# Splitting each query and key pair once on 128 partitions and stacking it by DMA inside SBUF, in a two-layer attention and ffn kernel

## The chip, the cores and the metric

One core of one Trainium2 chip. The metric is device time in microseconds (us) of one execution of the whole kernel, taken as the median of several runs; less is better.

## The reference, cut to what matters

A sequence of 512 tokens of width 1024 (batch 1) goes through two layers; each is an attention block and a gated ffn (width 2816, a causal convolution of three taps on the gate), each behind an rmsnorm and with a residual. Heads are 64 wide. Layer 0 has 8 FOX heads (causal attention with a learned decay added to the scores) and 8 DSA heads (keys and values from a shared latent of rank 128; a small indexer of 4 heads picks the keys that each query may see). Layer 1 has 16 MoBA heads, which at this length come to causal attention. For each head:

```python
s = jnp.einsum('bqhd,bkhd->bhqk', q_i, k) * scale          # FOX: + c_i - c_k
s = jnp.where(mask, s, -jnp.inf)                           # causal, or the picked keys
p = jax.nn.softmax(s, axis=-1)
out = jnp.einsum('bhqk,bkhd->bqhd', p, v)
```

All is float32, the result 512 x 1024.

## The kernel before, in words

Activations lie transposed: features on 128 partitions, 512 tokens along the columns. A float32 operand is kept as two TensorE operands, a high part (a cast to fp32r on ACT) and a low part (the operand minus its high part, on DVE or POOL); `split` (L125) makes both. A projection (`proj`, L160) is 8 tiles of the input by three products (high·high, high·low, low·high; L154 to L156), so 24 matmuls of 128x512. Its weights come by `chunk` (L131): a DMA on SP's queue (`raw_...`, L142, 512 KB, three buffers), a cast on ACT (L143), a subtraction on DVE (L149), or in layer 0's heads on POOL (L147).

Two heads make a pair: one projection gives q of both, head 0 on partitions 0 to 63 (`LO`), head 1 on 64 to 127 (`HI`); another gives k. A score product has only 64 rows to sum over, so the kernel fills all 128 partitions with it: q high above q low in one tile, k high twice in another, k low twice in a third, and two matmuls (L256, L257) give the sum of the four products. Tiles per pair: `stack_q` (L236) makes one for each head, `a` and `b`; `stack_k` (L245) makes `ah`, `al` for head 0 and `bh`, `bl` for head 1. q's parts are written where they belong, since ACT and DVE may write to other partitions than they read; k's are made on one half and copied to the other half by a DMA inside SBUF (L251), four for a pair. The indexer's `ik` (L510 to L514) is cast and subtracted twice, once for each half.

`soft` (L320) works a head's four blocks of 128 queries: scores into PSUM (two buffers), a masked copy with the row's maximum on DVE (L335, the `mx` rows), exp with the row's sum on ACT (L336), a reciprocal of the sum on DVE (L337), and the normalisation on POOL (L338). `mix` (L342) transposes the probabilities on PE (L358), splits them (L126, L127) and multiplies by the values (L367, L368).

`heads` (L444) sets the order in the program: the scores of a head, then some work for the next pair (`vals`, `ks`, `qs`: its value, key and query projections with their stacking), then `mix` of the head before. In layer 0 `select` puts rounds of DVE MAX8 and MATCH_REPLACE8 (L547, L548) among it. From this program order a scheduler makes an order for each engine and each queue, which the engines then follow strictly. In layer 1 there are eight pairs, `m0` to `m7`; their q is `mq`, their k `mk`, their values `mv` (`fq`, `fk`, `fv` of FOX; `dq`, `dk`, `dv` of DSA). The score of block 0 of pair 2, head 0 is `s_m20_0`.

Of the kernel before, what the change touches and what calls it, by code (L numbers as in the profile page):

```python
# [18 lines left out]
F32 = mybir.dt.float32  # L19
F32R = mybir.dt.float32r  # L20
I32 = mybir.dt.int32
AF = mybir.ActivationFunctionType
OP = mybir.AluOpType
# [4 lines left out]
NB = T // P  # L28
# [43 lines left out]
def hybrid_kernel(ctx: ExitStack, tc: tile.TileContext, xT_d, pos_d, const_d, vec_d, w_d, out_d, idx):  # L72
    nc = tc.nc
    V, A, G, PE = nc.vector, nc.scalar, nc.gpsimd, nc.tensor
# [7 lines left out]
    def big(name):  # L82
        return ap_.tile([P, T], F32R, tag="big", name=name, bufs=N_BIG)
# [7 lines left out]
    def col(name, n=1):  # L91
        return tp.tile([P, n], F32, tag=f"col{n}", name=name, bufs=N_COL)
# [32 lines left out]
    def split(dst_h, dst_l, src, eng=V):  # L125
        A.copy(dst_h, src)  # L126
        eng.tensor_tensor(dst_l, src, dst_h.bitcast(F32), op=OP.subtract)  # L127
# [101 lines left out]
    def halves(y, nm, eng=V):  # L229
        h, l = big(f"{nm}_h"), big(f"{nm}_l")  # L230
        split(h, l, y, eng)
        return h, l

    LO, HI = slice(0, 64), slice(64, 128)

    def stack_q(y, nm):  # L236

        a, b = big(f"{nm}_a"), big(f"{nm}_b")
        A.copy(a[LO], y[LO])
        A.copy(b[HI], y[HI])  # L240
        V.tensor_tensor(a[HI], y[LO], a[LO].bitcast(F32), op=OP.subtract)
        V.tensor_tensor(b[LO], y[HI], b[HI].bitcast(F32), op=OP.subtract)
        return a, b

    def stack_k(y, nm, eng=V):  # L245

        ks = [big(f"{nm}_{n}") for n in ("ah", "bh", "al", "bl")]
        for e, (r, q) in enumerate(((LO, HI), (HI, LO))):
            split(ks[e][r], ks[2 + e][r], y[r], eng)
            for t in (ks[e], ks[2 + e]):  # L250
                nc.sync.dma_start(t[q].bitcast(F32), t[r].bitcast(F32))  # L251
        return ks

    def scores(out, q, k, e, qs, w, first=True):

# [64 lines left out]
    def soft(nm, e, q, k, bias, decay=None):  # L320

        probs = []
        prt = tp.tile([P, P * NB * (NB + 1) // 2], F32, tag="prt", name=f"prt_{nm}", bufs=N_PR)
        for i in range(NB):
            w = P * (i + 1)
            wm = max(w, 256)
            s = ps("S", f"s_{nm}_{i}")
            qs = slice(i * P, i * P + P)
            if decay is not None:
                sel, ck = decay  # L330
                PE.matmul(s[:, :wm], sel.to_broadcast([P, P]), ck[:, :wm], start=True, stop=False)
            scores(s[:, :wm], q, k, e, qs, wm, decay is None)
            neg = prt[:, P * i * (i + 1) // 2:P * (i + 1) * (i + 2) // 2]
            mx, sm = col(f"mx_{nm}_{i}"), col(f"sm_{nm}_{i}")
            V.tensor_tensor_reduce(neg, s[:, :w], bias[i], scale=-0.125, scalar=3e38, op0=OP.add, op1=OP.min, accum_out=mx)  # L335
            A.activation(neg, neg, AF.Exp, scale=-1.0, bias=mx, accum_out=sm)  # L336
            V.reciprocal(sm, sm)  # L337
            G.tensor_scalar(neg, neg, sm, 1.0, op0=OP.mult, op1=OP.mult)  # L338
            probs.append(neg)
        return probs  # L340

    def mix(nm, e, probs, v, hv, y):  # L342
# [165 lines left out]

    ym = rope(pmisc, "misc")
    ikh, ikl = big("ik_h"), big("ik_l")  # L510
    A.copy(ikh[0:64], ym[0:64])
    A.copy(ikh[64:128], ym[0:64])
    V.tensor_tensor(ikl[0:64], ym[0:64], ikh[0:64].bitcast(F32), op=OP.subtract)
    V.tensor_tensor(ikl[64:128], ym[0:64], ikh[0:64].bitcast(F32), op=OP.subtract)  # L514
    kr = big("kr")
    G.memset(kr[0:64].bitcast(F32), 0.0)
    split(kr[64:96], kr[96:128], ym[64:96])
# [1 line left out]
    t = ps("T", "iwps")  # L519
# [32 lines left out]
    y = scaled(proj("ckv"), "ckv")  # L552
    sq = tmp("sqkv")
    A.activation(sq, y, AF.Square)
    _, bc = rstd_of(sq, P, "kv")
# [258 lines left out]
```

## Time and profile before

| | |
|---|---|
| median of 3 runs | 1278.89 us (1277.62 to 1280.02) |
| profiled execution, its own time | 1276.6 us |
| span of its instructions | 1274.8 us |
| mean granted clock of TensorE | 0.994 |
| PE busy | 1224.2 us (96%), 6148 matmuls |
| DVE busy | 845.7 us (66%) |
| ACT busy | 591.7 us (46%) |
| POOL busy | 311.0 us (24%) |

How to read it: the metric is the device time of an execution, the span runs from the first to the last instruction of the profiled execution. Busy times are of the engine's own instructions; a share of the whole span is an average over stages. The stages lie about so: setup and first norm to 52 us, the eight pairs of layer 0 to 262, its output projection and norm to 292, the ffn to 648, norm and first projections of layer 1 to 675, its eight pairs to 880, output projection and norm to 910, ffn to 1262, and the last norm and output.

### The profile page before, as it was taken

How to read it: one execution, taken by the hardware profiler on the slowest of the kernel's cores; microseconds unless marked ns; L12 is line 12 of the kernel's file. 1: busy time of each engine (PE TensorE's matmuls, PEld its weight loads, DVE VectorE, ACT ScalarE, POOL GpSimd, SP SyncE). 2: the span in 40 equal slices, each digit the busy share in tenths (PEclk: the TensorE clock that was granted, in tenths of full speed). 3: DMA queues.
4: the chain of work that ended last, by engine and by line, in shares of the span. 5: the costliest groups of instructions: out<-in, count | busy, mean ns of one | idle time of the engine just before them, and what ended most of it. 6: DMA issues, size and time to landing. Idle time of an engine off the chain costs nothing.

```text
span 1274.8 us, 17004 instructions
## 1 busy us (share of the span) xinstructions
PE 1224.2 (96%) x6148; PEld 1024.0 (80%) x6148; DVE 845.7 (66%) x1629; ACT 591.7 (46%) x1011; POOL 311.0 (24%) x354
## 2 busy tenths in 40 slices
PE   6899989999999999999999999999999999999996
PEld 4778767778888888888888788778788888888896
DVE  7899998776555345554467879787755533665564
ACT  5585667654333123333336556556433321333443
POOL 3586656541110001110114323222111100111000
PEclk9999999999999999999999999999999999999998
DMA  5223222222333233333323232222233333223363
GB/s 191 67 77 106 76 59 73 61 73 93 99 99 99 92 91 99 99 100 99 100 90 93 85 97 68 82 83 67 83 100 99 99 99 98 88 97 99 118 189 107
DMA packets 37379, 120.95 MB, mean 95 GB/s; under 512 B 4736, under 2 KB 4864, under 8 KB 37296
## 3 DMA queue, kind: packets, MB, share of 16 engines
q1 hardware_dynamic: 36368, 118.51, 30.4%
q10 hardware_dynamic: 864, 1.17, 0.3%
q8 instruction: 48, 0.79, 0.3%
q14 instruction: 35, 0.29, 0.1%
q0 software_dynamic: 64, 0.20, 0.0%
HBM read 109.37 MB, written 2.10 MB: 87 GB/s over the span
## 4 chain that ended last, share of the span: by engine, by line
PE 79%; DVE 14%; ACT 3%; issue 3%; POOL 0%; DMA 0%; DVEq 0%; ACTq 0%; POOLq 0%
PE mm_d L155 6%; PE mm_d L154 6%; PE mm_d L156 6%; PE mm_u L156 6%; PE mm_u L155 6%; PE mm_u L154 6%; PE mm_g L155 6%; PE mm_g L154 6%; PE mm_g L156 6%; DVE tmask L548 1%; DVE xl L170 1%; PE o_m L367 1%; DVE m L547 1%; PE t_m L358 1%; PE o_m L368 1%
## 5 line engine op out<-in xcount | busy, mean ns | idle before, releaser
L422 POOL TENSOR_TENSOR cv<-cv,sg 128x512 f32<-128x512 f32 x44 | 56.9, 1293 | 543.0 <-ACT sg L421 543.0
L155 PE MATMUL mm_d<-a_l,wh_d 128*128 128x512 f32 (+1 forms) x440 | 152.7, 347 | 0.0
L156 PE MATMUL mm_d<-a_h,wl_d 128*128 128x512 f32 (+1 forms) x440 | 152.5, 347 | 0.0
L154 PE MATMUL mm_d<-a_h,wh_d 128*128 128x512 f32 (+1 forms) x440 | 152.5, 347 | 0.0
L155 PE MATMUL mm_g<-xl,wh_g 128*128 128x512 f32 x352 | 137.1, 390 | 0.0
L156 PE MATMUL mm_u<-xh,wl_u 128*128 128x512 f32 x352 | 137.1, 390 | 0.0
L154 PE MATMUL mm_g<-xh,wh_g 128*128 128x512 f32 x352 | 136.9, 389 | 0.0
L154 PE MATMUL mm_u<-xh,wh_u 128*128 128x512 f32 x352 | 136.9, 389 | 0.0
L155 PE MATMUL mm_u<-xl,wh_u 128*128 128x512 f32 x352 | 136.9, 389 | 0.0
L156 PE MATMUL mm_g<-xh,wl_g 128*128 128x512 f32 x352 | 136.9, 389 | 0.0
L143 ACT CAST wh_d<-raw_d 128x1024 fp32r<-128x1024 f32 x55 | 57.8, 1050 | 122.4 <-PE mm_d L155 83.5
L149 DVE TENSOR_TENSOR wl_d<-raw_d,wh_d 128x1024 fp32r<-128x1024 f32 x55 | 67.6, 1229 | 66.7 <-ACT wh_d L143 66.5
L143 ACT CAST wh_u<-raw_u 128x1024 fp32r<-128x1024 f32 x44 | 46.4, 1054 | 131.6 <-PE mm_g L155 114.6
L154 PEld LDWEIGHTS mm_d<-a_h,wh_d 128*128 128x128 f32 x440 | 83.3, 189 | 10.4
L156 PEld LDWEIGHTS mm_d<-a_h,wl_d 128*128 128x128 f32 x440 | 83.3, 189 | 10.3
L155 PEld LDWEIGHTS mm_d<-a_l,wh_d 128*128 128x128 f32 x440 | 83.3, 189 | 10.2
L417 DVE TENSOR_TENSOR gs<-mm_g,RB 128x512 f32<-128x512 f32 x44 | 30.4, 692 | 90.7 <-PE mm_g L156 90.2
L424 DVE TENSOR_TENSOR us<-mm_u,RB 128x512 f32<-128x512 f32 x44 | 30.4, 692 | 81.2 <-PE mm_u L156 81.2
L154 PEld LDWEIGHTS mm_g<-xh,wh_g 128*128 128x128 f32 x352 | 66.1, 188 | 13.8
L154 PEld LDWEIGHTS mm_u<-xh,wh_u 128*128 128x128 f32 x352 | 66.1, 188 | 13.8
L155 PEld LDWEIGHTS mm_u<-xl,wh_u 128*128 128x128 f32 x352 | 66.1, 188 | 13.7
L156 PEld LDWEIGHTS mm_g<-xh,wl_g 128*128 128x128 f32 x352 | 66.1, 188 | 13.6
(775 smaller groups left out, 3080.2 us busy)
## 6 DMA issues: line engine op xcount, KB each, us to landing
raw_d<-in_w SPq DMA_DIRECT2D x55, 512.0 KB, 3.5
raw_g<-in_w SPq DMA_DIRECT2D x44, 512.0 KB, 3.5
raw_u<-in_w SPq DMA_DIRECT2D x44, 512.0 KB, 3.5
raw_oe<-in_w SPq DMA_DIRECT2D x8, 512.0 KB, 3.5
raw_mv<-in_w SPq DMA_DIRECT2D x8, 512.0 KB, 3.6
raw_mk<-in_w SPq DMA_DIRECT2D x8, 512.0 KB, 3.6
raw_mq<-in_w SPq DMA_DIRECT2D x8, 512.0 KB, 3.6
raw_oo<-in_w SPq DMA_DIRECT2D x8, 512.0 KB, 3.5
```

The lines of the kernel that those rows point to most:

```text
L143: A.copy(wh, raw)
L149: V.tensor_tensor(wl, raw, wh.bitcast(F32), op=OP.subtract)
L154: PE.matmul(out, ah, bh, start=first, stop=False)
L155: PE.matmul(out, ah, bl, start=False, stop=False)
L156: PE.matmul(out, al, bh, start=False, stop=last)
L170: V.scalar_tensor_tensor(xl[:, d], xT[:, d], gc, xh[:, d].bitcast(F32), op0=OP.mult, op1=OP.subtract)
L358: PE.transpose(t[:, n * P:n * P + P], probs[i][:, j * P:j * P + P], ident)
L367: PE.matmul(o[:, o0:o0 + w], vj, ph[:, c0:c0 + w], start=j == 0, stop=False)
L368: PE.matmul(o[:, o0:o0 + w], vj, pl[:, c0:c0 + w], start=False, stop=j == NB - 1)
L417: V.tensor_tensor(gs, og, RB, op=OP.mult)
L422: G.tensor_tensor(cv, cv, sg, op=OP.mult)
L424: V.tensor_tensor(us, ou, RB, op=OP.mult)
```

## The change

`stack_q` splits both heads at once on 128 partitions into `h` and `l` (one cast, one subtraction), and three DMAs inside SBUF put the parts where they belong: `a` gets head 0's high and low part, and head 1's high part is copied over head 0's low part in `l`, which so becomes the tile of head 1 (its high and low part swap places there). `stack_k` splits once too and makes `t` (head 0's key on both halves) and `b` (head 1's) by six DMAs: `b` twice from `t[HI]`, then `t[HI]` from `t[LO]`, once for the high and once for the low part. `ik` is split once on 64 partitions and copied by two DMAs. In `soft` the four row sums of a head lie in one tile of four columns; one reciprocal of 128x4 follows the fourth exp, and the four normalisations come after it.

```diff
--- before.py
+++ after.py
@@ -233,23 +233,28 @@
 
     LO, HI = slice(0, 64), slice(64, 128)
 
+    def move(dst, src):
+        nc.sync.dma_start(dst.bitcast(F32), src.bitcast(F32))
+
     def stack_q(y, nm):
 
-        a, b = big(f"{nm}_a"), big(f"{nm}_b")
-        A.copy(a[LO], y[LO])
-        A.copy(b[HI], y[HI])
-        V.tensor_tensor(a[HI], y[LO], a[LO].bitcast(F32), op=OP.subtract)
-        V.tensor_tensor(b[LO], y[HI], b[HI].bitcast(F32), op=OP.subtract)
-        return a, b
+        h, l = halves(y, nm)
+        a = big(f"{nm}_a")
+        move(a[LO], h[LO])
+        move(a[HI], l[LO])
+        move(l[LO], h[HI])
+        return a, l
 
     def stack_k(y, nm, eng=V):
 
-        ks = [big(f"{nm}_{n}") for n in ("ah", "bh", "al", "bl")]
-        for e, (r, q) in enumerate(((LO, HI), (HI, LO))):
-            split(ks[e][r], ks[2 + e][r], y[r], eng)
-            for t in (ks[e], ks[2 + e]):
-                nc.sync.dma_start(t[q].bitcast(F32), t[r].bitcast(F32))
-        return ks
+        out = []
+        for n, t in zip("hl", halves(y, nm, eng)):
+            b = big(f"{nm}_b{n}")
+            move(b[LO], t[HI])
+            move(b[HI], t[HI])
+            move(t[HI], t[LO])
+            out += [t, b]
+        return out[0], out[1], out[2], out[3]
 
     def scores(out, q, k, e, qs, w, first=True):
 
@@ -320,6 +325,7 @@
     def soft(nm, e, q, k, bias, decay=None):
 
         probs = []
+        sm = col(f"sm_{nm}", NB)
         prt = tp.tile([P, P * NB * (NB + 1) // 2], F32, tag="prt", name=f"prt_{nm}", bufs=N_PR)
         for i in range(NB):
             w = P * (i + 1)
@@ -331,12 +337,13 @@
                 PE.matmul(s[:, :wm], sel.to_broadcast([P, P]), ck[:, :wm], start=True, stop=False)
             scores(s[:, :wm], q, k, e, qs, wm, decay is None)
             neg = prt[:, P * i * (i + 1) // 2:P * (i + 1) * (i + 2) // 2]
-            mx, sm = col(f"mx_{nm}_{i}"), col(f"sm_{nm}_{i}")
+            mx = col(f"mx_{nm}_{i}")
             V.tensor_tensor_reduce(neg, s[:, :w], bias[i], scale=-0.125, scalar=3e38, op0=OP.add, op1=OP.min, accum_out=mx)
-            A.activation(neg, neg, AF.Exp, scale=-1.0, bias=mx, accum_out=sm)
-            V.reciprocal(sm, sm)
-            G.tensor_scalar(neg, neg, sm, 1.0, op0=OP.mult, op1=OP.mult)
+            A.activation(neg, neg, AF.Exp, scale=-1.0, bias=mx, accum_out=sm[:, i:i + 1])
             probs.append(neg)
+        V.reciprocal(sm, sm)
+        for i, neg in enumerate(probs):
+            G.tensor_scalar(neg, neg, sm[:, i:i + 1], 1.0, op0=OP.mult, op1=OP.mult)
         return probs
 
     def mix(nm, e, probs, v, hv, y):
@@ -508,10 +515,9 @@
 
     ym = rope(pmisc, "misc")
     ikh, ikl = big("ik_h"), big("ik_l")
-    A.copy(ikh[0:64], ym[0:64])
-    A.copy(ikh[64:128], ym[0:64])
-    V.tensor_tensor(ikl[0:64], ym[0:64], ikh[0:64].bitcast(F32), op=OP.subtract)
-    V.tensor_tensor(ikl[64:128], ym[0:64], ikh[0:64].bitcast(F32), op=OP.subtract)
+    split(ikh[LO], ikl[LO], ym[LO])
+    for t in (ikh, ikl):
+        move(t[HI], t[LO])
     kr = big("kr")
     G.memset(kr[0:64].bitcast(F32), 0.0)
     split(kr[64:96], kr[96:128], ym[64:96])
```

Counts by engine: DVE has 1431 instructions in its order where it had 1558, ACT 846 for 881, SP 369 DMAs for 281; PE keeps its 6148 matmuls. Three places of the order. First, SP's queue in layer 0, where the first FOX pair's q is stacked, in the order of the change (`fv1_0` is a weight chunk of the second value group, `fk2` and `fq2` are chunks of pair 2, `fk0` and `fq0` the tiles of pair 0).

```order
L142 DMA raw_fv1_0_1015<-in_w 128x1024
L142 DMA raw_fv1_1_1072<-in_w 128x1024
L237 DMA fk0_bh_669<-fk0_h_665 64x512 x2
L237 DMA fk0_bl_673<-fk0_l_666 64x512 x2
L142 DMA raw_fk2_1137<-in_w 128x1024
L237 DMA fk0_h_665<-fk0_h_665 64x512
L237 DMA fk0_l_666<-fk0_l_666 64x512
L142 DMA raw_fq2_1260<-in_w 128x1024
L237 DMA fq0_a_745<-fq0_h_741 64x512
L237 DMA fq0_a_745<-fq0_l_742 64x512
L237 DMA fq0_l_742<-fq0_h_741 64x512
```

The moves of `fq0` stand behind the load `raw_fq2`. In the order before, `fq0` needed no DMA, and `raw_fq2` stood behind the four copies of `fk0`.

Second, SP's queue in layer 1, where pair 2's q is stacked, in the order before:

```order
L251 DMA mk2_ah_6305<-mk2_ah_6305 64x512
L251 DMA mk2_al_6307<-mk2_al_6307 64x512
L251 DMA mk2_bh_6306<-mk2_bh_6306 64x512
L251 DMA mk2_bl_6308<-mk2_bl_6308 64x512
L142 DMA raw_mq4_6999<-in_w 128x1024
L142 DMA raw_mk5_7116<-in_w 128x1024
L251 DMA mk3_ah_6548<-mk3_ah_6548 64x512
L251 DMA mk3_al_6550<-mk3_al_6550 64x512
```

and in the order of the change:

```order
L237 DMA mq2_a_6339<-mq2_h_6335 64x512
L237 DMA mq2_a_6339<-mq2_l_6336 64x512
L142 DMA raw_mq4_6883<-in_w 128x1024
L142 DMA raw_mk5_6996<-in_w 128x1024
L237 DMA mq2_l_6336<-mq2_h_6335 64x512
L237 DMA mk3_bh_6452<-mk3_h_6448 64x512 x2
L237 DMA mk3_bl_6456<-mk3_l_6449 64x512 x2
L237 DMA mk3_h_6448<-mk3_h_6448 64x512
L237 DMA mk3_l_6449<-mk3_l_6449 64x512
```

The four copies of `mk3` were all that followed the loads `raw_mq4` and `raw_mk5`. Now the two moves that make `mq2_a` stand ahead of these loads, the one that makes head 1's tile `mq2_l` behind them.

On PE, the first score of that pair in the order before:

```order
L154 MATMUL mm_mk3_6517<-xh_74,wh_mk3_6512 128x512
L155 MATMUL mm_mk3_6517<-xl_75,wh_mk3_6512 128x512
L256 MATMUL s_m20_0_6475<-mk2_ah_6305,mq2_a_6431 128x256
L257 MATMUL s_m20_0_6475<-mk2_al_6307,mq2_a_6431 128x256
L367 MATMUL o_m10_6437<-pt_m10_0h_6438,mv0__5697 128x512
L256 MATMUL s_m20_1_6484<-mk2_ah_6305,mq2_a_6431 128x256
L257 MATMUL s_m20_1_6484<-mk2_al_6307,mq2_a_6431 128x256
L156 MATMUL mm_mk3_6517<-xh_74,wl_mk3_6513 128x512
L154 MATMUL mm_mk3_6517<-xh_74,wh_mk3_6512 128x512
```

and in the order of the change:

```order
L375 MATMUL o_m10_6343<-pt_m10_1l_6347,mv0__5621 128x384
L374 MATMUL o_m10_6343<-p3_0_0_92,mv0__5621 128x256
L365 MATMUL t_m11_0_6465<-const_70,prt_m11_6268 128x128 x4
L155 MATMUL mm_mq3_6537<-xl_75,wh_mq3_6532 128x512
L156 MATMUL mm_mq3_6537<-xh_74,wl_mq3_6533 128x512
L261 MATMUL s_m20_0_6382<-mk2_h_6215,mq2_a_6339 128x256
L262 MATMUL s_m20_0_6382<-mk2_l_6216,mq2_a_6339 128x256
L261 MATMUL s_m20_1_6388<-mk2_h_6215,mq2_a_6339 128x256
L375 MATMUL o_m10_6343<-p3_0_1_93,mv0__5621 128x256
L262 MATMUL s_m20_1_6388<-mk2_l_6216,mq2_a_6339 128x256
```

The first score stood inside the projection of `mk3`; now it stands inside that of `mq3`, the next one.

Third, DVE's queue over the softmax of the same head, in the order before:

```order
L337 RECIPROCAL sm_m20_0_6479<-sm_m20_0_6479 128x1
L335 ISA prt_m20_6474,mx_m20_2_6496<-s_m20_2_6493,cmask_81 128x384
L335 ISA mx_m20_2_6496 128x1
L127 TENSOR_TENSOR p3_0_1_93<-t_m10_2_6455,p3_0_0_92 128x128
L337 RECIPROCAL sm_m20_1_6488<-sm_m20_1_6488 128x1
L218 STREAM_SHUFFLE rs_mk3_6542<-mm_mk3_6517 128x512
L370 TENSOR_TENSOR y_m1_6111<-y_m1_6111,o_m10_6437 64x512
L337 RECIPROCAL sm_m20_2_6497<-sm_m20_2_6497 128x1
L335 ISA prt_m20_6474,mx_m20_3_6505<-s_m20_3_6502,cmask_81 128x512
L335 ISA mx_m20_3_6505 128x1
L219 TENSOR_TENSOR ry_mk3_6543<-mm_mk3_6517,CR_87 128x512
L149 TENSOR_TENSOR wl_mv2_1_6813<-raw_mv2_1_6811,wh_mv2_1_6812 128x1024
```

and in the order of the change:

```order
L341 ISA prt_m20_6381,mx_m20_1_6391<-s_m20_1_6388,cmask_81 128x256
L341 ISA mx_m20_1_6391 128x1
L341 ISA prt_m20_6381,mx_m20_2_6397<-s_m20_2_6394,cmask_81 128x384
L341 ISA mx_m20_2_6397 128x1
L218 STREAM_SHUFFLE rs_mk3_6442<-mm_mk3_6417 128x512
L377 TENSOR_TENSOR y_m1_6027<-y_m1_6027,o_m10_6343 64x512
L341 ISA prt_m20_6381,mx_m20_3_6403<-s_m20_3_6400,cmask_81 128x512
L341 ISA mx_m20_3_6403 128x1
L219 TENSOR_TENSOR ry_mk3_6443<-mm_mk3_6417,CR_87 128x512
L221 TENSOR_TENSOR ry_mk3_6443<-ry_mk3_6443,rs_mk3_6442 128x512
L344 RECIPROCAL sm_m20_6380<-sm_m20_6380 128x4
L127 TENSOR_TENSOR mk3_l_6449<-ry_mk3_6443,mk3_h_6448 128x512
```

Three of the four reciprocals of a column each are among the rows before; now one of four columns stands behind the last maximum, and `mk3_l` is one subtraction of 128x512 where `mk3_al` and `mk3_bl` were two of 64x512. The subtraction of `wl_mv2_1` was the last of these rows and is now ahead of them.

## Rows read from the trace of the kernel before

**Rows 1.** Windows: stretch, length, busy us (count) of PE, PEld, DVE, ACT, POOL; clock, DMA share, GB/s.

```profile
16.00:52.00 36.00, 31.24 (x152) 25.80 (x152) 32.53 (x68) 13.81 (x20) 14.68 (x16) 0.95 0.23 74
52.00:90.00 38.00, 34.68 (x188) 28.70 (x187) 33.77 (x96) 31.92 (x58) 28.26 (x31) 1.00 0.31 88
90.00:175.00 85.00, 80.82 (x462) 67.43 (x461) 80.35 (x224) 49.14 (x110) 53.23 (x72) 1.00 0.29 80
175.00:262.00 87.00, 82.15 (x425) 65.81 (x425) 69.76 (x197) 59.75 (x144) 49.92 (x71) 0.98 0.25 67
...
292.00:648.00 356.00, 355.89 (x1590) 295.38 (x1589) 185.24 (x222) 124.01 (x148) 36.99 (x28) 1.00 0.31 98
...
675.00:880.00 205.00, 199.63 (x1136) 168.62 (x1134) 166.30 (x404) 123.57 (x278) 64.16 (x78) 1.00 0.28 80
```

**Rows 2.** Waits of PE: who waited for whom, us in total, times, longest.

```profile
PE bc_n L199 <- DVE y_n L196: 6.4, 6, 3.0
...
PE s_m L256 <- DVE mq_a L241: 2.8, 4, 1.0
PE o_m L367 <- ACT pt_m_0h L126: 2.7, 4, 0.7
```

**Rows 3.** Groups of DVE in 52 to 262: count, busy us, mean ns, idle before.

```profile
L337 DVE RECIPROCAL sm_d<-sm_d 128x1 f32<-128x1 f32 x32 | 5.0, 158 | 0.5 <-ACT prt_d L336 0.3
L337 DVE RECIPROCAL sm_f<-sm_f 128x1 f32<-128x1 f32 x32 | 5.0, 156 | 0.2
...
L242 DVE TENSOR_TENSOR fq_b<-sc_fq,fq_b 64x512 fp32r<-64x512 f32 x4 | 4.3, 1080 | 0.1
...
L242 DVE TENSOR_TENSOR dq_b<-ry_dq,dq_b 64x512 fp32r<-64x512 f32 x4 | 3.7, 918 | 0.1
...
L127 DVE TENSOR_TENSOR dk_bl<-mm_dk,dk_bh 64x512 fp32r<-64x512 f32 x4 | 2.8, 694 | 0.2
```

**Rows 4.** Groups of DVE in 655 to 880.

```profile
L337 DVE RECIPROCAL sm_m<-sm_m 128x1 f32<-128x1 f32 x64 | 10.0, 158 | 2.4 <-ACT prt_m L336 1.9
...
L127 DVE TENSOR_TENSOR mk_bl<-ry_mk,mk_bh 64x512 fp32r<-64x512 f32 x8 | 6.2, 776 | 0.2
...
L242 DVE TENSOR_TENSOR mq_b<-ry_mq,mq_b 64x512 fp32r<-64x512 f32 x8 | 5.9, 735 | 0.3
...
L221 DVE TENSOR_TENSOR ry_mq<-ry_mq,rs_mq 128x512 f32<-128x512 f32 x8 | 5.5, 686 | 0.0
```

**Rows 5.** Groups of POOL in 52 to 262.

```profile
L127 POOL TENSOR_TENSOR fk_bl<-sc_fk,fk_bh 64x512 fp32r<-64x512 f32 x4 | 5.2, 1294 | 0.3
```

**Rows 6.** DMA issues (count, KB each, us to landing), and SP's timeline from 730.3.

```profile
mk_ah<-mk_ah SPq DMA_DIRECT2D x8, 128.0 KB, 3.2
...
mk_bl<-mk_bl SPq DMA_DIRECT2D x8, 128.0 KB, 3.0
...
dk_ah<-dk_ah SPq DMA_DIRECT2D x4, 128.0 KB, 4.8
...
730.89 0.47 SPq L251 DMA_DIRECT2D mk_ah<-mk_ah  x1
```

**Rows 7.** Timeline (start, length in us) of ACT and PE around pair 2's q, layer 1.

```profile
717.84 0.62 ACT L239 CAST mq_a<-ry_mq 64x512 fp32r<-64x512 f32 x1 [0.31 <-DVE ry_mq L221]
...
720.72 0.39 PE L256 MATMUL s_m<-mk_ah,mq_a 128*128 128x256 f32 x1 [0.62 <-DVE mq_a L241]
```

**Rows 8.** Timeline of POOL, DVE, PE and SP around the first FOX pair's q.

```profile
78.55 3.70 POOL L147 TENSOR_TENSOR wl_fv<-raw_fv,wh_fv 128x256 fp32r<-128x256 f32 x4
...
79.16 1.11 DVE L242 TENSOR_TENSOR fq_b<-sc_fq,fq_b 64x512 fp32r<-64x512 f32 x1
...
79.92 0.28 PE L256 MATMUL s_f<-fk_ah,fq_a 128*128 128x256 f32 x1
...
82.27 0.33 SPq L142 DMA_DIRECT2D raw_fq<-in_w  x1
```

**Rows 9.** Waits of SP's queue in 675 to 880.

```profile
SPq L142 <- DVE wl_mq L149: 33.4, 6, 9.1
```

## The prediction

> **What bounds the kernel now.** I read the table by windows first. Over the span TensorE (PE) is the bound: in the ffn it works 355.89 of 356 us, 1590 matmuls, 0.224 us each [rows 1]. Nothing that this change does to other engines can shorten that, since the matmuls stay. What can be won is PE's idle time where heads are worked: 36 − 31.24 = 4.8 us in 16 to 52 (setup of layer 0), 3.3 + 4.2 + 4.9 = 12.4 us in 52 to 262 (heads of layer 0), 205 − 199.63 = 5.4 us in 675 to 880 (heads of layer 1) [rows 1]. That is 22.6 us, the ceiling of any gain. In the same windows VectorE (DVE) is nearly as full: 80.35 of 85 us beside PE's 80.82 in 90 to 175, 166.30 of 205 in layer 1. So DVE can be what PE waits for there.
>
> The list of PE's waits says for what. The longest are norms (bc_n, 6.4 us), which the change doesn't touch. Of the heads: s_m for mq_a 2.8 us in 4 waits, o_m for pt_m_0h (a cast on ScalarE, ACT) 2.7 in 4 [rows 2]. No wait is long; the first of them is exactly the subtraction that the change rewrites.
>
> **The change, part by part.**
>
> *Work removed.* A cast or subtraction costs by its columns, not its partitions: 686 ns for ry_mq on 128x512, 735 for mq_b on 64x512 [rows 4]. So one split of 128 partitions replaces two of 64 at the price of one. In 52 to 262 DVE loses three quarters of the reciprocals (7.5 of 10.0 us; I take one of 128x4 at the price of one of 128x1, 0.16 us, since 128 columns of other work cost far less than 128 times that; at worst it costs four times as much and nothing is won), and the second subtraction of fq, dq and dk (4.3 + 3.7 + 2.8): 18.3 us of 184 [rows 1, 3]. In 655 to 880 it loses 7.5 + 6.2 + 5.9 = 19.6, beside 166 busy in 675 to 880 [rows 1, 4]. GpSimd (POOL) loses four subtractions of 1.29 us, one for each FOX pair [rows 5]. ACT loses 35 casts of some 0.62 us [rows 7]; it isn't the bound anywhere here.
>
> *Work added: moves.* q gets three DMAs, k six where it had four, ik two. SyncE (SP) issues them; in the trace one of 128 KB lands 3.2 us after its issue in layer 1 and 4.8 in the DSA pairs, and an issue takes SP 0.47 us [rows 6]. The third q move overwrites the source of the second, so it waits for its landing. The second head's l tile is then two landings behind the subtraction, the first head's a tile one.
>
> The Trainium skill, *SBUF — State Buffer*, "The DMA setup-cost knee", gives a transfer a fixed 2 us or so plus its bytes at 436 GB/s, an estimate of 2.3 us for 128 KB. The trace says 3.2 and decides; by 2.3 the two short pairs of layer 1 below would be about 0.9 us less short each, and the sum about 2 us lower.
>
> *16 to 52.* DVE loses three half-tile subtractions (iq twice, ik once), at 0.7 to 1.1 us each [rows 3, 4] 2 to 3 us of its 32.53. The moves of ik and iq have most of 24 us of matmuls between the projection and the first use (counted in the order). Named waits are mostly norms. I take **−1**; bounds −2.5 and +1.
>
> *Heads of layer 0.* A DVE relieved by 18.3 us can give back at most PE's 12.4 us of idle; the waits for DVE that I can name are short, so I take half, −6 (bounds 0 and −10). Against it, the first FOX pair: fq_b is done at 80.3 and the first score came at 79.92. After the change its moves stand behind raw_fq2, a load that waits for a buffer. It was issued at 82.27, when POOL had finished wl_fv (78.55 + 3.70) [rows 8]. POOL gets there 1.3 us earlier, so the load goes at 81.0, the moves at 81.3 and 81.9, and a is there at 85.1. The order puts the first score 12 matmuls later, 2.6 us, at 82.5: a wait of 2.6 us. The l move then lands near 88.9; the second head's first score stands 15 matmuls behind the first, at 88.4 or so: 0.5 more. Of these 3.1 I leave 2.5, since PE idled 3.3 us in this window anyway. The other seven pairs: q is ready some 3 us later (a landing plus an issue, less one subtraction), and the order gives fq1, fq2, fq3 and dq1 2.1 to 3.5 us more cover; dq0, dq2 and dq3 lose 0.6 to 3.8 of covers above 10 us. I allow +1.5 in all. Bounds of these costs 0 and +14 (the third rival). Together **−2**, from −8 to +8.
>
> *Heads of layer 1.* In the order before, 5.3 us of matmuls stand between the end of mq2's projection and its first score; the score then waited 0.62 us for mq_a [rows 7]. So q was ready 5.9 us after its projection. Now two moves are issued behind the subtraction (0.47 us each [rows 6]) and land (3.2): 10.1 us. The new order has 8.8, 8.5, 10.7, 11.4, 10.7, 11.4, 10.8 and 12.1 us of matmuls there for mq0 to mq7. Six pairs are covered; two are short by 1.3 and 1.6: 2.9 us come where the 2.8 of s_m for mq_a go. What is left is the waits for ACT (o_m, 2.7), relieved by a cast less in each split, and the rest of 5.4: I take **−2**. Bounds −5.4 and +5.
>
> *Moved without a price.* Later raw loads: in this layer SP spends 33.4 us in six mq loads waiting for a buffer [rows 9], so the loads run ahead of need, and a move or two in front costs nothing. The norms on POOL now all wait for the fourth exp; the transposes that read them mostly come several us later. If that cover is gone the price is some 1 us for each head, at most a few heads.
>
> **The sum.** −1 − 2 − 2 = **−5**: the profiled execution of 1276.6 would become 1271.6. It stood 2.3 below the median of the three runs, 1278.89, so the prediction is 1273.9. Its own range is 1271 to 1277.
>
> **The rivals.**
> 1. *DVE was the brake.* With 18.3 and 19.6 us off DVE, PE's waits for it go almost everywhere and the moves stay covered: −3, −6 and −4 of the ceilings, −13 + 2 for pair 0 = −11, 1267.9. For it: DVE at 95% in 90 to 175 beside PE at 95% [rows 1]. Against it: each named wait is short and much of the idle has other ends.
> 2. *Nothing net.* What the splits win, the late q's take: the waits for mq_a turn into waits for a move, and the selects and exps set the rest. 1278.9, give or take 2.6. For it: my own layer-1 account, 2.8 against 2.9.
> 3. *The queue, slower.* SP takes its DMAs in order. A load that waits for a buffer holds the q moves behind it, and such a load waits 33.4 / 6 = 5.6 us in the mean [rows 9]. In the order such a load stands in the way of all four FOX pairs' a tiles, and of the l tiles of mq2, mq4 and mq6. With 5.6 us of lateness against 2.1 to 3.5 of added cover, each loses some 2 to 3 us: 7 × 2 = 14, less 8 of gains, +6: 1284.9. It decides as soon as the loads' wait is longer than the cover that the order added. For it: rows 8 show it for the first pair. Against it: the scheduler put the scores back where it saw late moves, and a lighter DVE and POOL free buffers sooner.
>
> 4. *The moves go one after the other.* If the second move to a tile landed only a whole landing after the first, q would be ready not 10.1 but 12.8 us after its projection, and in layer 1 all eight pairs would be short, by 18.0 us in all instead of 2.9: 15 us more, 1289. Against it: the first and the last of mk's four copies, issued in a row, land after 3.2 and 3.0 us [rows 6].
>
> The Trainium skill, *DMA: Bandwidth & Descriptors*, "Rules for kernel authors", has this fourth case as a rule: two transfers to the two partition halves serialize, so one should not make them. By it the change would lose; rows 6 disagree, as far as a landing time can tell.
>
> **Chances.** A measurement of this kernel tells about 0.2%, 2.6 us, from no change. My forecast 0.40 (faster by more than that, mostly: 0.36), rival 1 0.15, rival 2 0.21, rival 3 0.22, rival 4 0.02. So faster 0.51, within 0.2% 0.25, slower 0.24. The range takes in rival 1 and the price of rival 3 with one more late pair: 1266 to 1286.
>
> **What would show it.** Right: DVE's busy time down by some 40 us, PE's waits for mq_a gone, a short wait of s_m for a DMA at pairs 0 and 1 and of 2 to 3 us of s_f at the first FOX pair, and PE's idle in 675 to 880 down to 3 or so. Wrong: PE waits of 2 us and more for moves at many pairs, with the issues of those moves right behind a raw load (rival 3); idle in 90 to 262 down by over 6 us (rival 1); or DVE not lighter.

## The result and the profile after

| | before | changed |
|---|---|---|
| median of five runs, same chip | 1277.77 us (1277.43 to 1280.02) | 1270.58 us (1268.13 to 1273.73) |
| profiled execution, its own time | 1276.6 us | 1268.1 us |
| span | 1274.8 us | 1266.3 us |
| mean granted clock of TensorE | 0.994 | 0.996 |

The ratio is 0.9943, 95% interval 0.9928 to 0.9958: 7.2 us faster. The forecast was 5 us faster (ratio 0.9961), and the measured time lies inside the stated range of 1266 to 1286 us; but the saving does not come from where the forecast put it, and the experiments show that it hangs on something that the forecast did not price, the order of the instructions.

The windows of the changed kernel (stretch, length, busy us and count of PE, PEld, DVE, ACT and POOL, clock, DMA share, GB/s), beside [rows 1]:

```profile
16.00:52.00 36.00, 30.84 (x168) 25.45 (x168) 31.62 (x76) 15.13 (x21) 14.68 (x16) 1.00 0.39 113
52.00:90.00 38.00, 33.41 (x174) 27.30 (x174) 33.07 (x89) 27.09 (x54) 28.37 (x32) 1.00 0.34 92
90.00:175.00 85.00, 80.53 (x463) 68.09 (x463) 79.04 (x205) 45.92 (x107) 47.07 (x68) 1.00 0.42 112
175.00:262.00 87.00, 86.71 (x457) 70.46 (x456) 62.63 (x161) 59.52 (x141) 53.48 (x75) 1.00 0.34 90
...
675.00:880.00 205.00, 200.24 (x1131) 171.67 (x1132) 152.73 (x332) 115.69 (x261) 60.74 (x78) 0.99 0.37 100
```

One stretch has gained clearly: 175 to 262, the DSA pairs. PE was idle there for 87 − 82.15 = 4.9 us and now is for 0.3, with DVE at 62.63 us instead of 69.76, and PE's granted clock is 1.00 there instead of 0.98, which is another 87 × 0.02 = 1.7 us by estimate. Most of that idle was made of waits for two results of DVE, and these are gone:

```profile
PE s_d L256 <- DVE mx_d L335: 2.3, 4, 1.0
...
PE mm_dk L623 <- DVE ry_dq L219: 1.5, 1, 1.5
```

In the FOX stretch, 52 to 175, PE is idle for more than before (9.1 us, 7.5 before), in layer 1 for about as much (4.8, 5.4 before). One row of the tile view for each kernel says when the first ffn begins, and so how much was saved ahead of it. Before:

```profile
L154 PE MATMUL mm_g<-xh,wh_g x352: 388/389/397, 280.0 to 1192.0; 128*128 128x512 f32 x176
```

and after the change:

```profile
L154 PE MATMUL mm_g<-xh,wh_g x352: 388/389/398, 271.4 to 1183.7; 128*128 128x512 f32 x176
```

The ffn's first gate projection begins 8.6 us earlier and the last one of the second ffn starts 8.3 us earlier: in this execution all of it is won ahead of the first ffn, and layer 1 adds nothing. PE's waits in the changed kernel:

```profile
PE bc_n L199 <- DVE y_n L196: 6.5, 6, 3.0
...
PE t_m L365 <- POOL prt_m L346: 2.6, 3, 1.7
PE s_f L261 <- DMA fq_a<-fq_l: 2.6, 1, 2.6
...
PE s_m L261 <- DMA mq_l<-mq_h: 1.8, 2, 1.2
...
PE s_m L261 <- DMA mq_a<-mq_l: 1.1, 1, 1.1
```

The waits of [rows 2] for mq_a and for the cast pt_m_0h are gone, the norm's (bc_n) stands as it was. In their place stand a wait of the FOX scores for q's move, 2.9 us of waits for mq's moves, and 2.6 of the transposes for the normalisation on POOL, which now begins behind the fourth exp.

The first FOX pair, in the timeline (start, length) of the changed kernel, beside [rows 8]:

```profile
74.89 3.29 POOL L147 TENSOR_TENSOR wl_fv<-raw_fv,wh_fv 128x256 fp32r<-128x256 f32 x4
...
76.18 0.70 DVE L127 TENSOR_TENSOR fq_l<-sc_fq,fq_h 128x512 fp32r<-128x512 f32 x1
...
78.20 0.33 SPq L142 DMA_DIRECT2D raw_fq<-in_w  x1
78.59 0.46 SPq L237 DMA_DIRECT2D fq_a<-fq_h  x1
79.10 0.59 SPq L237 DMA_DIRECT2D fq_a<-fq_l  x1
83.27 0.46 SPq L237 DMA_DIRECT2D fq_l<-fq_h  x1
...
83.30 0.38 PE L261 MATMUL s_f<-fk_h,fq_a 128*128 128x256 f32 x1 [2.60 <-DMA fq_a<-fq_l]
```

fq_l is done at 76.88, yet its moves are issued at 78.59, right behind the load raw_fq, which waited for POOL to finish wl_fv at 78.18. The second move lands 4.2 us after its issue, the third is issued then, and PE waits 2.60 us.

The costs of DVE's new instructions, in 52 to 262:

```profile
L127 DVE TENSOR_TENSOR fq_l<-sc_fq,fq_h 128x512 fp32r<-128x512 f32 x4 | 3.4, 859 | 0.0
...
L344 DVE RECIPROCAL sm_d<-sm_d 128x4 f32<-128x4 f32 x8 | 1.4, 172 | 1.2 <-ACT prt_d L342 1.2
L344 DVE RECIPROCAL sm_f<-sm_f 128x4 f32<-128x4 f32 x8 | 1.4, 169 | 0.6 <-ACT prt_f L342 0.5
```

A reciprocal of four columns takes 169 to 172 ns where one of one column took 156 to 158 [rows 3], and the one subtraction of fq, 128x512, takes 859 ns where that of one half took 1080. DVE's busy time fell from 845.7 to 815.4 us, ACT's from 591.7 to 568.2, POOL's from 311.0 to 300.5.

### The profile page after: what moved, and what is told of

Same layout as the page of the kernel before. It is cut to its first block, busy times and chain, and to the rows that moved or that the text cites. A ratio compares the mean times of both kernels' runs of the same rounds, so it can differ in the third digit from the quotient of the medians.

```text
span 1266.3 us, 16894 instructions
## 1 busy us (share of the span) xinstructions
PE 1218.5 (96%) x6148; PEld 1023.6 (81%) x6148; DVE 815.4 (64%) x1502; ACT 568.2 (45%) x976; POOL 300.5 (24%) x350
## 4 chain that ended last, share of the span: by engine, by line
PE 80%; DVE 11%; ACT 4%; issue 2%; DMA 2%; POOL 1%; SPq 0%; DVEq 0%; ACTq 0%; POOLq 0%
PE mm_d L156 6%; PE mm_d L154 6%; PE mm_d L155 6%; PE mm_u L156 6%; PE mm_u L154 6%; PE mm_u L155 6%; PE mm_g L154 6%; PE mm_g L156 6%; PE mm_g L155 6%; DVE tmask L554 2%; DVE m L553 1%; PE t_m L365 1%; PE mm_mk L154 1%; PE mm_mk L155 1%; PE mm_mk L156 1%
## 5 line engine op out<-in xcount | busy, mean ns | idle before, releaser
L155 PEld LDWEIGHTS mm_g<-xl,wh_g 128*128 128x128 f32 x352 | 66.1, 188 | 13.7
L156 PEld LDWEIGHTS mm_u<-xh,wl_u 128*128 128x128 f32 x352 | 66.1, 188 | 13.7
```

The lines of the kernel that those rows point to most:

```text
L155: PE.matmul(out, ah, bl, start=False, stop=False)
L156: PE.matmul(out, al, bh, start=False, stop=last)
```

## Experiments

Two readings stood against each other. **A**: VectorE (DVE) was the brake in layer 0 and the work taken from it is what pays. **D**: the scheduler makes another order out of the changed program, and this order is worth as much as the work. Each run has its own runs of the kernel before on the same chip beside it; the ratios are against those. "Idle in the DSA stretch" is 87 us less PE's busy time in 175 to 262.

### One layer at a time

The old functions were kept under other names (`stack_q_old`, `stack_k_old`, `soft_old`) and called in one layer. Layer 0 alone changed:

```diff
-                probs = soft(...)
+                probs = (soft_old if c['nm'][0] == 'm' else soft)(...)
-            c["q"] = stack_q(rope(proj(f"mq{p}"), f"mq{p}"), f"mq{p}")
+            c["q"] = stack_q_old(rope(proj(f"mq{p}"), f"mq{p}"), f"mq{p}")
-            c["k"] = stack_k(rope(proj(f"mk{p}"), f"mk{p}"), f"mk{p}")
+            c["k"] = stack_k_old(rope(proj(f"mk{p}"), f"mk{p}"), f"mk{p}")
```

> The change in layer 0 alone (setup, FOX and DSA heads); layer 1's heads are as before. Theory A (in the DSA pairs the queue of DVE was the brake, and layer 1 gives nothing): all of the gain is here, the span 8 to 9 us shorter than before, the median some 7 us lower, PE's idle in the stretch of the DSA pairs under 1 us. Rival B (the gain is the sum of small things all over, layer 1 too): 4 to 5 us lower, the rest missing. Rival C (the start at a fuller clock in the profiled execution made it): no more than 3 us lower.

Measured: ratio 0.9945 (0.9933 to 0.9957), 7.0 us faster. Its window of the DSA pairs:

```profile
175.00:262.00 87.00, 86.67 (x457) 70.43 (x456) 62.38 (x161) 60.18 (x144) 53.10 (x76) 1.00 0.35 92
```

The gain is layer 0's for the most part, and again 0.3 us of idle is left among the DSA pairs. The profiled span is 1269.8 us, 5.0 shorter than before's and not the 8 to 9 that A expected. Rival C falls: this execution's clock was 0.992, lower than before's 0.994, and the gain is there. Rival B expected less of layer 0, 4 to 5 us; what it said of layer 1 is the next run's.

The other half, layer 1 alone changed; the old functions are called for `iq`, `fq`, `fk`, `dq` and `dk`, and `ik` is made as before:

```diff
-                probs = soft(...)
+                probs = (soft if c['nm'][0] == 'm' else soft_old)(...)
-            c["q"] = stack_q(rope(proj(f"dq{p}"), f"dq{p}"), f"dq{p}")
+            c["q"] = stack_q_old(rope(proj(f"dq{p}"), f"dq{p}"), f"dq{p}")
...
-    split(ikh[LO], ikl[LO], ym[LO])
-    for t in (ikh, ikl):
-        move(t[HI], t[LO])
+    A.copy(ikh[0:64], ym[0:64])
...
```

> The change in layer 1 alone. Theory A: nothing within 2 us, since the waits for mq_a and for the cast pt_m_0h go and waits for q's moves and for the normalisation on POOL come in their place. Rival B: 2 to 4 us lower. My forecast's own term for it was 2 us lower.

Measured: 0.9984 (0.9976 to 0.9993), 2.0 us faster: my term for layer 1 stood. The value lies where A's "within 2 us" and B's "2 to 4" meet, so this run doesn't part the two. Its waits in that layer are those of the changed kernel:

```profile
PE s_m L279 <- DMA mq_l<-mq_h: 2.1, 2, 1.3
...
PE t_m L405 <- POOL prt_m L364: 1.8, 2, 1.5
```

That the changed kernel's own profiled execution shows no gain in layer 1 may be its clock there (0.99 in 675 to 880, 1.00 before): 1% of 205 us is 2 us. The two halves sum to 9.0 us, the interval of the whole reaches from 5.4 to 9.2.

### One part at a time

The one reciprocal alone, stacking as before:

```diff
+        sm = col(f"sm_{nm}", NB)
...
-            V.reciprocal(sm, sm)
-            G.tensor_scalar(neg, neg, sm, 1.0, op0=OP.mult, op1=OP.mult)
...
+        V.reciprocal(sm, sm)
+        for i, neg in enumerate(probs):
+            G.tensor_scalar(neg, neg, sm[:, i:i + 1], 1.0, op0=OP.mult, op1=OP.mult)
```

> Only the one reciprocal for a head; stacking as before. Theory A (gain by DVE time taken away where the selects run): it takes 7.5 of the 18.3 us that the whole change takes from DVE in layer 0's heads, so about 3 us there; in layer 1 the transposes wait for the normalisation (2.6 us in the changed kernel), so 0 to 3 us lower in all. Rival D (the gain is in the order that the scheduler happened to make, not in the work): no relation to the share, anything from 4 slower to 7 faster, and DVE's idle in the DSA pairs not changed as the work is.

Measured: 1.0020 (1.0011 to 1.0028), 2.6 us slower. A took it for 0 to 3 us faster and is wrong here. D allowed anything from 4 slower to 7 faster, so the run supports it only weakly. PE's busy time in the DSA stretch was 81.29 us, 5.7 idle, and in layer 1 it waits longer for ACT than before (2.7 us in [rows 2]):

```profile
PE o_m L369 <- ACT pt_m_0h L126: 3.6, 4, 1.5
```

The stacking alone, with the four reciprocals (the inverse of that diff, applied to the changed kernel):

> The stacking by DMA with the four reciprocals as before. Theory A: 10.8 of the 18.3 us of DVE still go, so 4 to 5 us lower in layer 0; layer 1 is without the waits for POOL's normalisation, 1 to 2 us better than in the changed kernel; 5 to 7 us lower in all. Rival D: no relation to the share. Rival E (the reciprocal is what matters, since it is what ties DVE to ACT's exps): 2 us lower at most.

Measured: 0.9999 (0.9989 to 1.0009), nothing, where A wanted 5 to 7 us. Rival E (the reciprocal is what matters) is within its bound of 2 us here, but it has the run before against it, in which the reciprocal alone is slower. The trace shows the price that the forecast's third rival had named, at three pairs. SP's queue and PE at the second FOX pair:

```profile
100.54 0.33 SPq L142 DMA_DIRECT2D raw_fq<-in_w  x1
101.00 0.46 SPq L237 DMA_DIRECT2D fq_a<-fq_h  x1
101.50 0.60 SPq L237 DMA_DIRECT2D fq_a<-fq_l  x1
...
105.88 0.36 PE L261 MATMUL s_f<-fk_h,fq_a 128*128 128x256 f32 x1 [1.84 <-DMA fq_a<-fq_h]
```

and PE's waits for those moves over the whole kernel:

```profile
PE s_f L261 <- DMA fq_a<-fq_h: 4.8, 2, 2.9
...
PE s_f L261 <- DMA fq_a<-fq_l: 2.9, 1, 2.9
```

Three FOX pairs wait 7.7 us for q's moves. In the changed kernel one does, for 2.6: in its order the second pair's moves stand ahead of raw_fq. So four reciprocals for a head or one, operations that have nothing to do with these queues, decide through the order whether three pairs wait or one. The 5.1 us between the two are not all that this run lost against the changed kernel: its heads of layer 0 also wait 1.9 us for a normalisation on POOL (t_d for prt_d) and 1.9 for a cast (o_d for pt_d_0h), which the changed kernel doesn't, and PE's clock from 90 to 175 was 0.94 in this execution, 1.00 in that of the changed kernel (it is one of this kernel's slower executions, 1282.4 us).

The change with q's stacking as before (two casts, two subtractions, no moves of q):

```diff
-        h, l = halves(y, nm)
-        a = big(f"{nm}_a")
-        move(a[LO], h[LO])
-        move(a[HI], l[LO])
-        move(l[LO], h[HI])
-        return a, l
+        a, b = big(f"{nm}_a"), big(f"{nm}_b")
...
+        return a, b
```

> The change with the stacking of q as before: no moves of q, two casts and two subtractions for it. Theory A with the queue's price (late q in the FOX pairs): DVE in layer 0's heads loses 10.3 us instead of 18.3, the wait of 2.6 us for the first FOX pair's move goes, and in layer 1 those of 2.9 for mq's moves: 5 to 8 us lower than before. Rival F (q's stacking is what pays, since it shortens the chain to the scores by a cast and a subtraction): 3 us lower at most.

Measured: 0.9986 (0.9977 to 0.9994), 1.8 us faster: no late q, and yet 5 us less than the changed kernel. The DSA stretch has 87 − 82.91 = 4.1 us of idle. The expectation's first theory falls; F's bound holds, but the run with stacking alone makes the full change to q and gains nothing, so F's reason is not shown by it.

### Less work for DVE, the rest alone

Half of the selection rounds of the last block of queries left out, so that it picks other keys, first in the kernel before:

```diff
-        for _ in rounds:
+        for _ in rounds[:0] if i == 3 and rounds.start else rounds:
```

> The kernel before, but the last block of queries (384 to 511) gets only 8 of its 16 rounds of key selection: 8 MAX8 and 8 MATCH_REPLACE8 of 128x512 less, 8 x (0.68 + 0.68) = 10.9 us of DVE, all in the stretch where the DSA pairs begin; it computes another set of keys there. Nothing else is touched. Theory A (DVE was the brake there): PE's 4.9 us of idle in 175 to 262 go for the most part, 3 to 6 us lower. Rival D (the order decides): less than 1.5 us either way.

Measured: 0.9964 (0.9952 to 0.9977), 4.6 us faster, the size that A expected, but not by the way that A named. PE's idle among the DSA pairs, which was to go for the most part, only fell from 4.9 to 3.8 us:

```profile
175.00:262.00 87.00, 83.21 (x440) 66.84 (x438) 67.03 (x185) 59.63 (x140) 47.90 (x70) 1.00 0.24 68
```

The clock is 1.00 there instead of 0.98, and 0.995 in the mean of this kernel's five timed runs where the runs of the kernel before beside them have 0.993: by estimate 1278 × (0.9954 − 0.9930), some 3 of the 4.6 us. So this run doesn't show that DVE's load was the brake; what the kernel before waited for are the single instructions in its rows above. The same in the changed kernel:

> The changed kernel with the same 8 rounds left out. Theory A: the changed kernel has 0.3 us of idle on PE left in the DSA pairs, so DVE is no longer the brake and 10.9 us less of its work bring 0 to 1.5 us on top of the change. Rival D: no prediction; as much as in the kernel before would speak against A.

Measured: 1.0002 (0.9989 to 1.0016). With 10.9 us of DVE work less than the changed kernel it is 7.5 us slower than it. No account by work can give that. Its DSA stretch and the waits in it:

```profile
175.00:262.00 87.00, 81.97 (x427) 66.05 (x426) 58.28 (x151) 53.99 (x132) 48.02 (x69) 0.98 0.32 90
```

and PE's waits from 175 to 275:

```profile
PE o_d L374 <- ACT pt_d_0h L126: 2.9, 2, 2.5
PE mm_dq L154 <- DVE dv L127: 2.0, 1, 2.0
```

DVE is busy 58.28 us of 87, the least so far, and PE is idle for 5.0 us: it waits for single instructions (the cast of the probabilities, the split of the values) that stand late in their engine's queue, not for an engine without time. That reading is mine, from these rows; the next runs test it.

### The same instructions in another order

This led to the run that tells A from D. The first eight rounds of selection of two blocks come one place later in the program, nothing else:

```diff
-            w[1:1] = [lambda n=n: select(n - 1, range(8))]
+            w[2:2] = [lambda n=n: select(n - 1, range(8))]
```

> The changed kernel with the first 8 selection rounds of the last two blocks one place later in the program (behind the query projection instead of ahead of it): the same instructions in another order, layer 1 the same row for row. Theory A (the work taken from DVE is what pays): within 2 us of the changed kernel, so 5 to 8 us lower than before. Rival D (the order that the scheduler makes is worth as much as the work): 3 to 7 us off the changed kernel, most likely slower, with waits of PE in the DSA pairs for casts and subtractions, as where rounds were left out.

Measured: 1.0002 (0.9992 to 1.0013). The whole gain is gone. Its DSA stretch and its waits there:

```profile
175.00:262.00 87.00, 81.52 (x428) 65.20 (x426) 58.65 (x156) 56.35 (x140) 50.72 (x73) 0.98 0.34 87
```

and PE's waits from 175 to 275:

```profile
PE mm_dq L154 <- DVE dv L127: 2.9, 1, 2.9
PE s_d L261 <- DMA dq_a<-dq_l: 1.6, 1, 1.6
PE o_d L374 <- ACT pt_d_0h L126: 0.7, 2, 0.4
```

The waits are of the same kind as in the run with fewer rounds. The same shift in the kernel before:

> The same shift in the kernel before. Theory A: within 2 us of before. Rival D: 3 to 7 us off it, either way.

Measured: 1.0003 (0.9994 to 1.0011), no difference: that is what A expected, and D, which wanted 3 to 7 us, misses here. In its trace PE is idle for 5.1 us among the DSA pairs (4.9 before), and for 9.0 in 52 to 175 (7.5 before); the clock, 0.995 in the mean of its timed runs for 0.993, gives this back, by estimate some 2 us. And once more in the changed kernel, the second value group of DSA one place earlier (between key and query projection of its pair):

```diff
-        return c, [ks, qs] + ([vals] if p % 2 == 0 else [])
+        return c, ([ks, vals, qs] if p == 2 else [ks, qs] + ([vals] if p % 2 == 0 else []))
```

> The changed kernel with the second DSA value group computed between key and query projection of its pair instead of behind them: again the same instructions in another order, and layer 1 unchanged. Rival D, which the shifted selection rounds favoured: anywhere from 0 to 9 us lower than before, and whichever it is, the difference to the changed kernel lies between the FOX pairs' last mixes and the end of the DSA pairs. If it keeps the 7 us of the changed kernel, the shifted selection was a bad order rather than the changed one a lucky one.

Measured: 1.0041 (1.0026 to 1.0056), 5.2 us slower than before and 12 slower than the changed kernel, with the same work. The difference is of the kind that D expects, but its way is not: D said 0 to 9 us lower than before. In the DSA stretch:

```profile
175.00:262.00 87.00, 78.71 (x403) 64.06 (x403) 56.89 (x149) 52.92 (x131) 51.01 (x73) 0.96 0.33 85
```

8.3 us of idle, where the changed kernel has 0.3. So of three orders of the changed kernel's work one is 7 us faster than before, one equal, one 5 slower. The changed work brought the gain in one order and not in two others, as D has it, though D was wrong on the shift in the kernel before and on the direction of the last run. What is left of A is that the kernel before did wait for DVE there, for single results; the changed kernel is rid of these waits only if the order lets it. How much of the 7.2 us the lighter DVE made possible was not separated from the order.

### Another queue, and a better version

q's moves on ACT's queue:

```diff
-        move(a[LO], h[LO])
-        move(a[HI], l[LO])
-        move(l[LO], h[HI])
+        for d, s in ((a[LO], h[LO]), (a[HI], l[LO]), (l[LO], h[HI])):
+            nc.scalar.dma_start(d.bitcast(F32), s.bitcast(F32))
```

> The changed kernel with q's three moves on ACT's queue instead of SP's, so that no weight load stands ahead of them. Theory G (a load that waits for its buffer holds up q): the waits of s_f and s_m for moves (2.6 and 2.9 us) shrink by more than half, 2 to 4 us lower than the changed kernel. Rival H (what makes q late is the two landings, not the queue): no change, or slower by up to 3 us, since ACT now waits for DVE's subtraction and for a landing before its next cast.

Measured: 1.0114 (1.0098 to 1.0130), 14.6 us slower, more than H allowed. PE's longest waits in layer 1:

```profile
PE s_m L260 <- DMA mq_a<-mq_l: 4.0, 2, 2.4
PE s_m L260 <- issue: 2.9, 3, 1.1
PE o_m L373 <- ACT p L126: 2.3, 1, 2.3
```

PE waits for the moves still, and now for ACT's casts behind them as well. That fits a queue in which the moves hold up ACT while they wait for DVE's subtraction and for a landing; which of the two costs more was not measured. G's forecast of 2 to 4 us less than the changed kernel is wrong. With no load ahead of them q's moves are no longer what the FOX scores wait for (they wait 3.8 us for a move of k instead), but those of layer 1 are, longer than in the changed kernel (4.0 us for 1.1 at mq_a), so ACT's queue is no cure.

At last a version with what each layer showed: layer 0 as changed, in layer 1 the stacking by DMA with the four reciprocals.

```diff
-                probs = soft(...)
+                probs = (soft4 if c['nm'][0] == 'm' else soft)(...)
```

> Layer 0 as changed; layer 1 with the stacking by DMA but the four reciprocals as before. From the profiles so far layer 1's heads gain about 3 us by the stacking and lose 3 by the one reciprocal (the normalisation on POOL comes late). If that holds (theory I): 2 to 4 us lower than the changed kernel, about 10 lower than before, with no wait of t_m for prt_m left. Rival D (order): 0 to 3 us slower than the changed kernel.

Measured: 0.9927 (0.9913 to 0.9941), 9.3 us faster than before; against the changed kernel's 0.9943 the intervals overlap, so the 2 us between them are likely and not shown by the times. By the traces, the stretch of layer 1 from the last matmul of mk0's projection to the last of the values (o_m) took 215.5 us before, 218.4 with the one reciprocal alone, 213.6 in the run with layer 1 alone changed, and 212.4 both here and in the run with stacking alone. In the changed kernel's own execution it took 215.6, at the lower clock named above. The waits of t_m for prt_m fell from 2.6 to 1.2 us but did not vanish. In the DSA stretch:

```profile
175.00:262.00 87.00, 85.88 (x460) 69.89 (x460) 61.94 (x165) 59.13 (x148) 50.65 (x73) 1.00 0.38 100
```

1.1 us of idle: the order of the changed kernel, kept in layer 0, keeps its gain there.

| run | faster (−) or slower, us | PE idle in 175 to 262, us | mean clock of its runs |
|---|---|---|---|
| layer 0, and layer 1 with four reciprocals | −9.3 | 1.1 | 0.994 |
| changed kernel | −7.2 | 0.3 | 0.993 |
| layer 0 alone | −7.0 | 0.3 | 0.993 |
| before, fewer rounds | −4.6 | 3.8 | 0.995 |
| layer 1 alone | −2.0 | 4.8 | 0.993 |
| q stacked as before | −1.8 | 4.1 | 0.992 |
| stacking alone | −0.1 | 7.3 | 0.991 |
| kernel before | 0 | 4.9 | 0.993 |
| changed, fewer rounds | +0.3 | 5.0 | 0.990 |
| changed, selection shifted | +0.3 | 5.5 | 0.990 |
| before, selection shifted | +0.4 | 5.1 | 0.995 |
| one reciprocal alone | +2.6 | 5.7 | 0.994 |
| changed, values shifted | +5.2 | 8.3 | 0.988 |
| q's moves on ACT's queue | +14.6 | 6.7 | 0.987 |

The second column is 1278 times the ratio less one (for the changed kernel the difference of the medians), the third is 87 us less PE's busy time in that window of the one profiled execution, the fourth is PE's granted clock, mean over the timed runs. The window cuts a little more or less of the neighbouring work in each kernel, and runs differ in layer 1 too. The second and third go together roughly, with exceptions, and neither goes with the amount of work taken from DVE.

The clock is a part of the price that idle time leaves out. In the run with the values shifted, PE's clock fell from 2.4 to 1.2 GHz right behind two of its waits,

```profile
209.99 0.50 PE L374 MATMUL o_d<-pt_d_0h,dv 128*128 128x512 f32 x1 [1.94 <-ACT pt_d_0h L126]
...
217.05 0.36 PE L261 MATMUL s_d<-dk_h,dq_a 128*128 128x256 f32 x1 [2.33 <-DMA dq_a<-dq_h]
```

as the windows behind them show (0.50 is the lower level, 1.00 the higher):

```profile
210.50:213.50 3.00, 3.00 (x11) 2.48 (x11) 2.03 (x4) 0.94 (x3) 3.00 (x5) 0.50 0.34 66
217.50:220.50 3.00, 3.00 (x11) 2.66 (x11) 1.89 (x7) 1.68 (x5) 0.00 (x0) 0.50 0.79 179
221.00:225.00 4.00, 4.00 (x25) 3.45 (x23) 1.66 (x5) 2.37 (x5) 2.66 (x4) 1.00 0.15 33
```

PE is busy throughout these and gets 11 matmuls, of mixed sizes, done in 3 us, then 25 in 4. Not every wait is followed by such a fall: behind the 2.60 us of the changed kernel at 83.30 the clock stayed at 1.00. By an estimate from the last column, the values shifted lost 1278 × (0.993 − 0.988), some 6 of their 12 us against the changed kernel, by the clock, and the selection shifted some 4 of its 7.5. The changed kernel's own gain over before is not the clock's: its runs have 0.993, as those of the kernel before.

## Why the prediction was right, and where it was not

**The sum** was right in sign and size: −5 forecast, −7.2 measured (−9.2 to −5.4). As a time, 1270.58 lies 0.4 us below the forecast's own 1271 to 1277 and about midway between it and rival 1's 1267.9; taken from the 1278.89 that the forecast started from, the ratio gives 1271.6. Rivals 2 and 4 did not come, and rival 1's sign, idle in 90 to 262 down by over 6 us, did not either: it went from 9.0 to 4.8. That the sum came out so near is in part luck, as two of its terms show:

- *Setup, −1.* The first FOX key projection starts 2.7 us earlier in the changed kernel's profile (57.6 for 60.3), but part of it is the clock, 1.00 against 0.95 in that window [rows 1]; in three later profiles of the same setup code with 0.95 (selection shifted, values shifted, four reciprocals in layer 1) it starts 1.5 to 2.0 us earlier. Somewhat undersized.
- *Heads of layer 0, −2.* This is the term that was mis-sized: together with the setup −3, against 7.0 measured in the run with layer 0 alone. The step was "I take half, −6" of PE's idle for a lighter DVE. In 52 to 262 the idle did not halve, it fell from 12.4 to 9.4 us: all of it went in the DSA pairs (4.9 to 0.3), while the FOX pairs got 1.6 us more. In the same executions the way from the first FOX key projection to the first gate projection is 5.9 us shorter; another 1.7 of these are the clock in the DSA stretch, and the rest has no row of its own. The ceiling of 22.6 us of idle was for the same reason not a ceiling: the clock can be won back too. What the step left out is what decides it: not how much DVE has to do, but which instruction stands where in its queue when PE needs it. That the same work gives −7.2, 0.3 and +5.2 us in three orders means that no sum over durations could have told this term; its honest bounds were about those that I gave, −8 to +8, and the middle of them was a choice. That the changed kernel's order was one of the good ones is luck.
- *First FOX pair.* The wait of 2.6 us came as 2.60, but that it agrees to the digit is luck, by steps that erred both ways: the load went at 78.20 instead of 81.0, because POOL was not one but four microseconds ahead, the score was due earlier too (80.7 instead of 82.5), and the move landed after 4.2 us instead of 3.2. The 0.5 us of the second head did not show as a wait.
- *Heads of layer 1, −2.* As measured alone, 2.0 (0.9 to 3.1), with the trade that the term had named: 2.8 us of waits for mq_a against 2.9 for its moves. But only 1.1 of these are at a short first head, that of pair 0; the other 1.8 are at the second heads of pairs 2 and 4, whose tile mq_l stands behind loads and to whose lateness this term gave no price. PE's idle in 675 to 880 was to fall to 3 or so and is 4.8 in that execution. What I had put at "some 1 us for each head, at most a few heads" as the price of a late normalisation is real: 2.6 us of waits of t_m, and the one reciprocal alone costs that stretch 2.9 us. The stacking alone gains it 3.1.
- *Rival 3* (the queue) did not decide the changed kernel, but it is the largest named part of what took the gain from the stacking alone: three FOX pairs behind a waiting load, 7.7 us. It was the right mechanism with too low a sense of how the order picks between one pair and three.
- *The prices.* One reciprocal of four columns at that of one: 0.17 against 0.16. A split of 128 partitions at the price of one half: right. DVE's busy time was to fall by some 40 us and fell by 30.3; the page of the profile doesn't count twice what overlaps. Added up one by one, the durations of all DVE instructions fell by 37.6 us (913.9 to 876.3).

*SBUF — State Buffer*, "The DMA setup-cost knee", of the Trainium skill gave the estimate of 2.3 us for a move, the trace of before 3.2. The first two of the changed kernel's moves of q in layer 1 land in 2.2, the first of those of k in 3.2, as its DMA issues show (KB each, us to landing):

```profile
mk_bh<-mk_h SPq DMA_DIRECT2D x16, 128.0 KB, 3.2
...
mq_a<-mq_h SPq DMA_DIRECT2D x8, 128.0 KB, 2.2
mq_a<-mq_l SPq DMA_DIRECT2D x8, 128.0 KB, 2.2
```

So the page's estimate holds for the moves of mq_a, and the row that I took holds for those of mk. What makes the difference was not tested: to stand in a row of four is not enough, since those of the DSA keys land in 2.3 to 2.4 (dk_bh, dk_bl). The fourth rival finds no support: the two halves of mq_a land after 2.2 us each, the second no later than the first. For the rule in *DMA: Bandwidth & Descriptors*, "Rules for kernel authors", of the Trainium skill, that transfers to two partition halves serialize, this tells no more than that the second is not a whole landing late; the two moves of a pair are issued 0.6 us or more apart there.

What stays open: why exactly the changed order leaves no wait in the DSA pairs. The runs show that the order does it and which waits come back in other orders; which of the moved instructions is the one that matters was not tried. Nor was the clock held apart from the order: it falls behind some waits and not behind others.

## What to carry to other kernels

Where a scheduler orders the engines' queues anew after every edit, a measured gain belongs to the edit and its order together: shift something neutral by a place and run again before you credit the edit. Take the idle time of the stretch, and what it runs below full clock, as what can be won, and look at which single instructions end the waits there; the work removed from a busy engine says little. Look at where in its queue a DMA stands that must follow an engine's result: here it cost up to 7.7 us of waits behind loads that waited for buffers, and on the queue of ACT, for which others wait, the kernel became 14.6 us slower than before.

## What was not expected of the hardware

A reciprocal of 128x4 took 169 to 173 ns where one of 128x1 took 156 to 158, so the four cost some 14 ns more than the one. Moves of 128 KB inside SBUF landed between 2.2 us (mq_a) and 4.4 us (fk_bh) after their issue in the medians of the changed kernel. In the run with the values shifted, waits of 1.94 and 2.33 us were each followed by a stretch at a granted clock of 0.50, so that by the matmuls done in it they cost more than their own length; a wait of 2.60 us in the changed kernel was not.
